# One ring of raw weight tiles for the last gate/up block and the first down group, with the forms reloaded earlier and evictions in the results' tiles

## The chip, the cores and the metric

The kernel runs on 1 core of one Trainium2 chip. The metric is the device time of one execution in microseconds. Before the change it is 1963.46 us, the median of 3 runs (1961.62 to 1964.4).

## The reference, cut to what matters

The input is one sequence of 512 tokens by 2048 features in float32. The layer is an input projection, two attention mixers, an output projection, and then a SwiGLU feed-forward block; a final RMSNorm follows. The change touches only the feed-forward block, and its last part:

```
h2 = rmsnorm(x, g_ffn[layer])
gate, up = jnp.split(jnp.einsum('bsd,df->bsf', h2, w_gate_up[layer]), 2, axis=-1)
x = x + jnp.einsum('bsf,fd->bsd', jax.nn.silu(gate) * up, w_down[layer])
```

`w_gate_up` is 2048 by 11264 and `w_down` 5632 by 2048, both float32.

## The kernel before

**Arithmetic.** A float32 product is made of three matmuls on rounded halves (L227 to L229: high by high, high by low, low by high). So each weight tile needs a high part, which ACT writes (L836), and a low part, which DVE writes as the tile less its high part (L839). Large products use a seven-product scheme: of four blocks of weights it makes seven combinations, called forms, m1 to m7, worked through in the order m1, m7, m6, m2, m5, m4, m3. The combinations of weights are sums on DVE (L972, here called the sum). The activations' forms lie in two tiles that stay in SBUF, `arena2` (two forms) and `arena5` (five).

**Gate/up.** Eleven blocks, each of 56 units: 7 forms by 8 units, where a unit is six matmuls. Two units share one sum and one split, and are called a duo here. So a form has the duos 0 to 3. A block loads 28 raw weight tiles of 512 KB by SyncE's queue (L272). They are named here by form and duo: a0 to a3 (for m1), c0, b0, ..., c3, b3 (m7; m6 is made of the same tiles), d0 to d3 (m2), e0 to e3 (m5, which sums e with a), f0 to f3 (m4, which sums f with b), g0 to g3 (m3). The eight tiles a and b stay in SBUF from m1 or m7 to m5 or m4, since these sums are written into them.

**Rings.** The raw tiles of gate/up block 1 to 9 come from a ring of 12 places, tag `craw`: a place goes to the next raw tile in the order in which places came free. A raw place is free when the split to its low part (L839) or the sum that read it (L972) is done. Block 10, the last one, has a ring of its own with 10 places, tag `craw40`, and the first down group another of 10 places, tag `draw6`.

**Loading.** The kernel is planned unit by unit: `prepare(n)` stands ahead of unit n, and issues loads (`load_raws`), high splits, sums and low splits as far ahead as rings and times allow. All weight loads go in the order of their use on one queue, so a load that waits holds the loads behind it.

**Results of a gate/up block.** Products are copied (`snap`), added (L1228), passed through SiLU and multiplied; the outcome is transposed by DMA (L1257), merged by ACT into a tile `pair` (L1263), summed there by DVE into forms (L378), and stored to DRAM by GpSimd's queue (L1266, 896 KB, in two halves per block). The second half of block 9 is stored in block 10, and the second half of block 10 in the first down group. In block 10 these results lie in general slots, in the other blocks in tiles of their own.

**Down.** Three groups of weight rows (6, 8 and 8 pairs), each by two column blocks. In group 1 a column block has 42 units and 24 raw loads; its loads are named D.0, D.1 and so on here. `next_forms` brings the activations' forms back from DRAM ahead of each group: a load on ACT's queue (L1306, 512 KB for four pairs), a high split on ACT (L1309) and a low split on DVE (L1312), each form's at a turn counted in units. An eviction copies a result bank with ACT (L1333) and adds it to DRAM by a GpSimd DMA (L1334). Its tiles are a ring of six, tag `ev`.

Of the kernel before, what the change touches and what calls it, by code (L numbers as in the profile page):

```python
# [11 lines left out]
F32 = mybir.dt.float32  # L12
# [8 lines left out]
P = 128  # L21
# [4 lines left out]
KD = D // P  # L26
# [23 lines left out]
SPILLED = {"A": 4, "B": 6}  # L50
TWINS = 8
WIDE = 4
WIDE_AHEAD = 9.5
RAWS = {"raw": 6, "craw": 12, "craw1": 24, "craw0": 24, "kraw": 9, "craw40": 10, "draw6": 10, "draw8": 15}
KEPT_TAGS = ("craw",)
W_TILES = {"wi": 10, "wo": 12}
DOWN_PAIRS = (6, 8, 8)
ORDER = ("m1", "m7", "m6", "m2", "m4", "m5", "m3")
# [1 line left out]
EVICT = 6  # L60
# [15 lines left out]
def encoder_block(ctx, tc, x, w_in, g_q_a, g_k_a, w_out, w_gate_up, w_down, g_final, x_t, gains, c_ident, c_mask,  # L76
# [15 lines left out]
    def slot(base, dtype=F32, shape=(P, 512)):  # L92
        return sp.tile(list(shape), dtype, tag="s", name=nm(base))
# [25 lines left out]
    stage = wp.tile([P, 20, 512], F32, tag="stage", bufs=1, name="stage")  # L119
    homes = deque(stage[:, n] for n in range(8, 20))  # L120
    homing = [True]
    kept_raws = deque()
    extra_homes, retired = {}, []

    def more_homes(name, tile):
# [109 lines left out]
    twins, evs, frs = [], [], []  # L235
# [965 lines left out]
    held = {}  # L1201

    def hold(name, shape, dtype=F32):
        if name not in held:
            held[name] = sp.tile([P] + list(shape), dtype, tag=name, bufs=1, name=nm(name))
        return held[name]

    forms_dram = dp.tile([P, 7, NFF // 2, 256], F32, tag="forms", name="forms")
    def gate_up_block(f0):
        box = ColBlock(w_gate_up, 0, (f0 * P, DFF + f0 * P), KD // 2, REREAD, "craw40" if f0 == 40 else "craw", hf if f0 == 0 else None, two=True)  # L1210
        st = {}

        def tile2(name):
            st[name] = [slot(name) if f0 == 40 else hold(f"{name}{t}", [512]) for t in range(2)]
            return st[name]

        def snap(form, name):
# [60 lines left out]
        for n, late in enumerate((3, 4, 6, 7)):  # L1278
            box.after("m3", late, lambda n=n: planes(("glo", "uhi")[n // 2], n // 2, n % 2))
            box.after("m3", late + 7, lambda n=n: turn(n))  # L1280
        for j, late in enumerate((23, 50 if f0 == 40 else 36)):
            for n, part in enumerate(((1, 0, 4, 1024), (0, 2, 4, 0), (0, 0, 2, 256))):
                box.after("m3", late + n, lambda j=j, part=part: merge(j, *part))
            box.after("m3", late + 3, lambda: pair_sums(hpart[0]))
            box.after("m3", late + 5, lambda j=j: store(f0 // 2 + j))
        return box

    for f in range(0, NFF, 4):
        box = gate_up_block(f)

    def load_x1(c, rows):
        for t in rows:
# [3 lines left out]
    def next_forms(box, first, pairs):  # L1296
        seq, turns = sorted(CHAIN, key=box.at.get), [0]

        def ready(form, h):
            m, st = ORDER.index(form), {}  # L1300
            lo_q, n = 4 * h, min(4, pairs - 4 * h)
            hi, lo = (form_tile(m, slice(lo_q, lo_q + n))[:, :, j] for j in range(2))

            def load():
                st["t"] = in_turn(frs, 2, [P, 4, 256], F32, "fr")[:, :n]
                nc.scalar.dma_start(st["t"], forms_dram[:, m, first + lo_q:first + lo_q + n])  # L1306

            def split_hi():
                nc.scalar.activation(hi, st["t"], AF.Copy)  # L1309

            def split_lo():
                nc.vector.tensor_tensor(lo, st["t"], f32(hi), op=OP.subtract)  # L1312
            turn = max(box.at[form] + 4 * seq.index(form) + 4 * h + 1, turns[-1] + 4)
            turns.append(turn)
            hook(turn - 5, load)
            hook(turn, split_hi)
            hook(turn + 2, split_lo)
        for form in seq:
            for h in range(-(-pairs // 4)):
                ready(form, h)  # L1320
# [3 lines left out]
    def down_block(first, pairs, cb, last):  # L1324
# [3 lines left out]
        def add(form, i, j):  # L1328
            def go():
                for t in range(2):  # L1330
                    row = 2 * i + t
                    e = in_turn(evs, EVICT, [P, 512], F32, "ev")
                    nc.scalar.activation(e, box.bank_of(form)[t], AF.Copy, scale=r2["r"][:, row:row + 1])  # L1333
                    nc.gpsimd.dma_start(x1_dram[2 * cb + j, row], e, accum_op=OP.add)  # L1334
                if form in LAST_OF_BANK:
                    box.done(form)
            box.after(form, 0, go)
# [129 lines left out]
    def load_raws(n):  # L1467
        while done["load"] < len(units) and at[done["load"]] <= at[n] + units[done["load"]].load_ahead:
            for raw in units[done["load"]].raws:
                if raw.t is None:  # L1470
                    for r in live:
                        if last_use[r] < done["lo"] and r.homed and homing[0] and not any(r.t is h for h in retired):
                            homes.append(r.t)
                        elif last_use[r] < done["lo"] and not homing[0] and r.tag in KEPT_TAGS:
                            kept_raws.append(r.t)
                    live[:] = [r for r in live if last_use[r] >= done["lo"]]
                    if homing[0] and len(homes) <= (2 if xs[KD - 1] is None else 4 if done["load"] < 24 else 0):
                        return
                    if homing[0] and raw.tag == "raw" and sum(r.tag == "raw" for r in live) >= 2:
                        return  # L1480
                    if sum((r.tag == "raw") == (raw.tag == "raw") for r in live) >= RAWS[raw.tag]:
                        return
                    live.append(raw)
                    raw.load()
            done["load"] += 1
# [115 lines left out]
```

## Time and profile before

| | us |
|---|---|
| median of 3 runs | 1963.46 |
| the profiled execution | 1962.45 |
| its span | 1960.7 |
| TensorE busy in it | 1940.9 |
| VectorE busy in it | 1537.2 |
| ScalarE busy in it | 1129.3 |

The mean granted clock was 0.996. The first matmul of gate/up block 9 starts at 1368.07 us of the span, of block 10 at 1444.23, of the first column block of down group 1 at 1526.21, of its second at 1583.37, and of down group 2 at 1647.16. Matmuls overlap in the records, so that a unit's length is read from start to start. A weight load row (`raw`) starts at its issue; the chain of waits counts it until it lands.

### The profile page before, as it was taken

Reading aid. Unit: us, or ns where it says so; the run is one execution under the profiler, and the core shown is the slowest. Engines: PE = TensorE matmul, PEld = TensorE weight load, DVE = VectorE, ACT = ScalarE, POOL = GpSimd, SP = SyncE. Lnnn points to the kernel's source line nnn. Section 1 sums busy time; section 2 is a strip of 40 time slices with the busy share of each in tenths; the row PEclk is TensorE's granted clock in tenths of the full one; section 3 lists DMA queues with packets and bytes.
Section 4 is the critical chain, followed back from the end, with each engine's and each line's share of the span. In section 5 each row is a group of like instructions: output and inputs, shape, how many; then the busy total and the mean of one; then the engine's idle time right before and its main releaser. Section 6 shows DMA issues by size and latency. Waiting matters only on the chain.

```text
span 1960.7 us, 24582 instructions
## 1 busy us (share of the span) xinstructions
PE 1940.9 (99%) x8727; PEld 1600.7 (82%) x8727; DVE 1537.2 (78%) x2012; ACT 1129.3 (58%) x1649; POOL 140.2 (7%) x184
## 2 busy tenths in 40 slices
PE   9999999999999999999999999999999999999998
PEld 7888888888888888888888888888887887888886
DVE  7987778887775697778778778778787877787886
ACT  7655554565455565555555555555555656555555
POOL 1000011000000000000000000000000121111121
PEclk9999999999999999999999999999999999999999
DMA  9777693144342466858758757767678789868865
GB/s 345 236 258 236 210 280 108 59 145 156 102 151 97 172 209 188 295 150 274 262 151 284 242 173 278 224 197 283 200 231 288 202 220 296 225 157 252 225 146 167
DMA packets 256252, 410.35 MB, mean 209 GB/s; under 512 B 62912, under 2 KB 90048, under 8 KB 256000
## 3 DMA queue, kind: packets, MB, share of 16 engines
q1 hardware_dynamic: 225296, 322.17, 50.5%
q0 software_dynamic: 22480, 60.57, 12.4%
q10 hardware_dynamic: 8352, 26.05, 4.0%
q8 instruction: 68, 1.11, 0.2%
q14 instruction: 56, 0.46, 0.1%
HBM read 334.52 MB, written 62.65 MB: 203 GB/s over the span
## 4 chain that ended last, share of the span: by engine, by line
PE 91%; DVE 4%; issue 2%; DMA 2%; ACT 1%; POOL 0%; SPq 0%; DVEq 0%; POOLq 0%; ACTq 0%
PE b L229 29%; PE b L228 29%; PE b L227 29%; PE b L612 1%; DMA raw<-in_w_gate_up_dram 1%; DVE wide L839 1%; POOL x1d L1334 0%; PE b L1170 0%; DVE raw L972 0%; PE b L562 0%; DMA forms<-pair 0%; DMA raw<-in_w_in_dram 0%; DVE x L1124 0%; DMA raw<-in_w_down_dram 0%; DVE w L305 0%
## 5 line engine op out<-in xcount | busy, mean ns | idle before, releaser
L836 ACT ACTIVATE wide<-raw 128x1024 fp32r<-128x1024 f32 x462 | 487.2, 1059 | 474.3 <-PE b L229 265.7
L228 PE MATMUL b<-wide,arena 128*128 128x512 f32 x1848 | 721.4, 390 | 4.4 <-DVE wide L839 4.4
L227 PE MATMUL b<-wide,arena 128*128 128x512 f32 x1848 | 721.2, 390 | 3.1 <-ACT wide L836 2.5
L839 DVE TENSOR_TENSOR wide<-raw,wide 128x1024 fp32r<-128x1024 f32 x462 | 562.5, 1223 | 205.2 <-ACT wide L836 195.7
L229 PE MATMUL b<-wide,arena 128*128 128x512 f32 x1848 | 721.0, 390 | 0.0
L228 PEld LDWEIGHTS b<-wide,arena 128*128 128x128 f32 x1848 | 347.9, 188 | 77.8 <-DVE wide L839 5.6
L227 PEld LDWEIGHTS b<-wide,arena 128*128 128x128 f32 x1848 | 348.0, 188 | 76.0 <-ACT wide L836 2.9
L229 PEld LDWEIGHTS b<-wide,arena 128*128 128x128 f32 x1848 | 348.0, 188 | 72.6
L972 DVE TENSOR_TENSOR raw<-raw,raw 128x1024 f32<-128x1024 f32 x264 | 321.5, 1220 | 11.9 <-DMA raw<-in_w_gate_up_dram 11.8
L228 PE MATMUL b<-tw,arena 128*128 128x512 f32 x396 | 154.3, 390 | 0.6 <-DVE tw L895 0.6
L229 PE MATMUL b<-tw,arena 128*128 128x512 f32 x396 | 154.2, 389 | 0.0
L227 PE MATMUL b<-tw,arena 128*128 128x512 f32 x396 | 154.1, 389 | 0.0
L892 ACT ACTIVATE tw<-stage 128x512 fp32r<-128x512 f32 x140 | 85.5, 628 | 69.4 <-DVE stage L972 45.0
L895 DVE TENSOR_TENSOR tw<-stage,tw 128x512 fp32r<-128x512 f32 x140 | 93.9, 688 | 22.0 <-ACT tw L892 21.2
L218 ACT ACTIVATE pTh<-b 128x512 fp32r<-128x512 f32 x64 | 38.2, 597 | 101.0 <-PE b L612 95.7
L227 PE MATMUL b<-w,arena 128*128 128x512 f32 x240 | 95.8, 399 | 0.0
L229 PE MATMUL b<-w,arena 128*128 128x512 f32 x240 | 93.9, 391 | 0.0
L228 PE MATMUL b<-w,arena 128*128 128x512 f32 x240 | 93.5, 390 | 0.0
L1334 POOL DMA_DIRECT2D x1d<-ev x76 | 66.0, 962 | 318.0 <-ACT ev L1333 295.3
L378 DVE TENSOR_TENSOR pair<-pair 128x256 f32<-128x256 f32 x120 | 46.6, 422 | 53.6 <-ACT pair L1263 29.4
L228 PEld LDWEIGHTS b<-tw,arena 128*128 128x128 f32 x396 | 74.3, 188 | 16.8 <-DVE tw L895 1.5
L229 PEld LDWEIGHTS b<-tw,arena 128*128 128x128 f32 x396 | 74.3, 188 | 15.8 <-DVE arena L346 0.4
(229 smaller groups left out, 2107.0 us busy)
## 6 DMA issues: line engine op xcount, KB each, us to landing
raw<-in_w_gate_up_dram SPq DMA_DIRECT2D x308, 512.0 KB, 6.1
raw<-in_w_down_dram SPq DMA_DIRECT2D x88, 512.0 KB, 6.9
stage<-in_w_in_dram SPq DMA_DIRECT2D x111, 256.0 KB, 5.3
forms<-pair POOLq DMA_DIRECT2D x22, 896.0 KB, 8.2
x1d<-ev POOLq DMA_DIRECT2D x76, 256.0 KB, 6.2
fr<-forms ACTq DMA_DIRECT2D x35, 512.0 KB, 6.2
raw<-in_w_out_dram SPq DMA_DIRECT2D x32, 512.0 KB, 4.2
stage<-in_w_in_dram SPq DMA_DIRECT2D x90, 128.0 KB, 3.4
```

What stands on the lines that cost most here:

```text
L218: nc.scalar.activation(hi, src, AF.Copy)
L227: nc.tensor.matmul(dst, ah, bh, start=start, stop=False, skip_group_check=chained)
L228: nc.tensor.matmul(dst, ah, bl, start=False, stop=False, skip_group_check=chained)
L229: nc.tensor.matmul(dst, al, bh, start=False, stop=stop, skip_group_check=chained)
L378: nc.vector.tensor_tensor(out, x, y, op=op)
L612: nc.tensor.transpose(ps[:, t * P:(t + 1) * P], self.p[t][:, kb * P:(kb + 1) * P], ident)
L836: nc.scalar.activation(self.hi, self.src, AF.Copy)
L839: nc.vector.tensor_tensor(self.lo, self.src, f32(self.hi), op=OP.subtract)
L892: nc.scalar.activation(self.pair[:, 0], self.src, AF.Copy)
L895: nc.vector.tensor_tensor(self.pair[:, 1], self.src, f32(self.pair[:, 0]), op=OP.subtract)
L972: nc.vector.tensor_tensor(t[dst], t[src[0]], t[src[1]], op=OP.add if form == "m6" else OP.subtract)
L1334: nc.gpsimd.dma_start(x1_dram[2 * cb + j, row], e, accum_op=OP.add)
```

## The change

The last block and down group 1 take their raw tiles from the ring `craw` too, which is 12 places at first and 10 from unit 22 of block 10 on: two places that come free then are dropped. The results of every block lie in the results' own tiles (`s1`, `s7`, `s6` and so on, each of two halves), and the evictions use the six halves of `s1`, `s6` and `s7` in place of the ring `ev`. The first group's forms are reloaded from unit 24 of block 10 on at the earliest, every four units. The second merge of block 10 stands 40 units behind the start of m3's evictions, not 50. The ring `draw8` has 16 places instead of 15.

```diff
+RELOAD_AT = 24
+RELOAD_STEP = 4
+DROP_AT = 22
-RAWS = {"raw": 6, "craw": 12, "craw1": 24, "craw0": 24, "kraw": 9, "craw40": 10, "draw6": 10, "draw8": 15}
-KEPT_TAGS = ("craw",)
+RAWS = {"raw": 6, "craw": 12, "craw1": 24, "craw0": 24, "kraw": 9, "craw40": 10, "draw6": 10, "draw8": 16}
+KEPT_TAGS = ("craw", "craw40", "draw6")
...
-    kept_raws = deque()
+    kept_raws, dropped = deque(), [0]
...
-            st[name] = [slot(name) if f0 == 40 else hold(f"{name}{t}", [512]) for t in range(2)]
+            st[name] = [hold(name, [2, 512])[:, t] for t in range(2)]
...
-        for j, late in enumerate((23, 50 if f0 == 40 else 36)):
+        for j, late in enumerate((23, 40 if f0 == 40 else 36)):
...
+    last_gate = box.at["m1"] - KD // 2 + 1
...
             turn = max(box.at[form] + 4 * seq.index(form) + 4 * h + 1, turns[-1] + 4)
+            if first == 0:
+                turn = max(box.at[form] + 1, box.at["m1"] + RELOAD_AT, turns[-1] + RELOAD_STEP)
...
-                    e = in_turn(evs, EVICT, [P, 512], F32, "ev")
+                    if not evs:
+                        evs.extend(held[name][:, t] for name in ("s1", "s6", "s7") for t in range(2))
+                    evs.append(evs.pop(0))
+                    e = evs[-1]
...
-                            kept_raws.append(r.t)
+                            if n >= last_gate + DROP_AT and dropped[0] < RAWS["craw"] - RAWS["draw6"]:
+                                dropped[0] += 1
+                            else:
+                                kept_raws.append(r.t)
...
-                    if sum((r.tag == "raw") == (raw.tag == "raw") for r in live) >= RAWS[raw.tag]:
+                    most = RAWS["craw"] if raw.tag == "craw40" and n < last_gate + DROP_AT else RAWS[raw.tag]
+                    if sum((r.tag == "raw") == (raw.tag == "raw") for r in live) >= most:
```

The number of instructions on each engine stays the same, and so does the order on TensorE and SyncE. Lines of the kernel's body stand three to eleven lower after the change: L272, L839 and L972 become L275, L842 and L975, L1266 becomes L1269, L1312 becomes L1317, and L1334 becomes L1344.

The first place is the weight loads on SyncE in m2 and m5 of block 10. Before, these eight rows are the loads d2, d3, e0, e1, e2, e3, f0 and f1; every raw tile has a name of its own, and the pool gives it its place.

```order
L272 DMA raw_571_10949<-in_w_gate_up_dram 128x2x512
L272 DMA raw_572_10967<-in_w_gate_up_dram 128x2x512
L272 DMA raw_575_10990<-in_w_gate_up_dram 128x2x512
L272 DMA raw_576_11012<-in_w_gate_up_dram 128x2x512
L272 DMA raw_577_11031<-in_w_gate_up_dram 128x2x512
L272 DMA raw_578_11033<-in_w_gate_up_dram 128x2x512
L272 DMA raw_579_11050<-in_w_gate_up_dram 128x2x512
L272 DMA raw_580_11052<-in_w_gate_up_dram 128x2x512
```

After the change the same eight loads on SyncE go to tiles of the ring, so a name that comes again is a place used again.

```order
L275 DMA raw_518_5788<-in_w_gate_up_dram 128x2x512
L275 DMA raw_534_5886<-in_w_gate_up_dram 128x2x512
L275 DMA raw_539_5961<-in_w_gate_up_dram 128x2x512
L275 DMA raw_534_5886<-in_w_gate_up_dram 128x2x512
L275 DMA raw_536_5908<-in_w_gate_up_dram 128x2x512
L275 DMA raw_539_5961<-in_w_gate_up_dram 128x2x512
L275 DMA raw_512_5739<-in_w_gate_up_dram 128x2x512
L275 DMA raw_534_5886<-in_w_gate_up_dram 128x2x512
```

The place of d2 (`raw_518`) is not used again, and e1 goes where d3 was (`raw_534`), e2 to the place of a0 (`raw_536`), into which the sum of e0 is written, e3 to e0's place (`raw_539`), f0 to a1's (`raw_512`), f1 to e1's.

The second place is DVE in the same stretch. Before the change this is what stands there, from the sum of e0 (out in a0's tile, `raw_551`) to the split of e2's sum.

```order
L972 TENSOR_TENSOR raw_551_10632<-raw_575_10990,raw_551_10632 128x1024
L839 TENSOR_TENSOR wide_532_5847<-raw_572_10967,wide_531_5846 128x1024
L1312 TENSOR_TENSOR arena2_84<-fr_562_10790,arena2_84 128x2x256
L972 TENSOR_TENSOR raw_552_10648<-raw_576_11012,raw_552_10648 128x1024
L839 TENSOR_TENSOR wide_526_5841<-raw_551_10632,wide_525_5840 128x1024
L972 TENSOR_TENSOR raw_553_10664<-raw_577_11031,raw_553_10664 128x1024
L839 TENSOR_TENSOR wide_528_5843<-raw_552_10648,wide_527_5842 128x1024
L972 TENSOR_TENSOR raw_554_10680<-raw_578_11033,raw_554_10680 128x1024
L839 TENSOR_TENSOR wide_530_5845<-raw_553_10664,wide_529_5844 128x1024
```

After the change DVE has this there, again from the sum of e0 (out in `raw_536`) on.

```order
L975 TENSOR_TENSOR raw_536_5908<-raw_539_5961,raw_536_5908 128x1024
L842 TENSOR_TENSOR wide_532_5847<-raw_534_5886,wide_531_5846 128x1024
L975 TENSOR_TENSOR raw_512_5739<-raw_534_5886,raw_512_5739 128x1024
L842 TENSOR_TENSOR wide_526_5841<-raw_536_5908,wide_525_5840 128x1024
L975 TENSOR_TENSOR raw_538_5940<-raw_536_5908,raw_538_5940 128x1024
L842 TENSOR_TENSOR wide_528_5843<-raw_512_5739,wide_527_5842 128x1024
L975 TENSOR_TENSOR raw_537_5938<-raw_539_5961,raw_537_5938 128x1024
L842 TENSOR_TENSOR wide_530_5845<-raw_538_5940,wide_529_5844 128x1024
```

The low split of d3 (out of `raw_534`) is the second row, and e1 (third row) comes into that same tile behind it; the split of e0's sum (fourth row) is the last reader of `raw_536` before e2 is loaded there, and the sum of e2 is the row behind. The reload (L1312) between the first rows is gone from here. Further on in the same stretch, DVE after the change has these rows, from the split of f2's sum (`raw_524`) to that of g0:

```order
L842 TENSOR_TENSOR wide_530_5845<-raw_524_5838,wide_529_5844 128x1024
L1231 TENSOR_TENSOR s7_545_6137<-b7_78,s7_545_6137 128x512
L1231 TENSOR_TENSOR s7_545_6137<-b6_77,s7_545_6137 128x512
L1317 TENSOR_TENSOR arena2_84<-fr_548_10972,arena2_84 128x4x256
L842 TENSOR_TENSOR wide_532_5847<-raw_535_5906,wide_531_5846 128x1024
L842 TENSOR_TENSOR wide_526_5841<-raw_537_5938,wide_525_5840 128x1024
```

Before the change the two adds of this place (L1228) are followed by the split of f3's sum with no reload (L1312) between. The third place is GpSimd's queue at the turn from the first to the second column block of down group 1, where the store of the last forms stood among the evictions like this:

```order
L1334 DMA x1d11_127<-ev_598_11376 128x512
L1334 DMA x1d20_130<-ev_599_11377 128x512
L1334 DMA x1d21_131<-ev_600_11378 128x512
L1334 DMA x1d32_136<-ev_601_11379 128x512
L1334 DMA x1d33_137<-ev_602_11380 128x512
L1266 DMA forms_138<-pair_467_5381 896x1x256
```

After the change the same stretch of GpSimd's queue reads:

```order
L1344 DMA x1d11_127<-s1_544_6071 128x512
L1269 DMA forms_138<-pair_467_5381 896x1x256
L1344 DMA x1d20_130<-s6_546_6203 128x512
L1344 DMA x1d21_131<-s6_546_6203 128x512
L1344 DMA x1d32_136<-s7_545_6137 128x512
L1344 DMA x1d33_137<-s7_545_6137 128x512
```

The store of the `pair` tile now stands ahead of the first two evictions of the second column block. In this column block the load D.22 went to the place of `pair` before (tile `raw_615`); now it goes to the ring's `raw_538`, which the low split of the sum of a down unit reads last, and D.24 is the first load at a place of the next group's ring.

## The prediction

> **What bounds the kernel now.** I read the page's first part, then the busy time by block, TensorE's waits, and the chain of waits around the two places where it waits. The page, and TensorE's waits summed over the run (us in total, times, longest):
>
> ```profile
> span 1960.7 us, 24582 instructions
> PE 1940.9 (99%) x8727; PEld 1600.7 (82%) x8727; DVE 1537.2 (78%) x2012; ACT 1129.3 (58%) x1649; POOL 140.2 (7%) x184
> ...
> PE b L228 <- DVE wide L839: 4.4, 3, 3.5
> PE b L227 <- ACT wide L836: 2.5, 1, 2.5
> ```
>
> TensorE is the bound. Only time in which it waits, or runs at a lower clock, can be gained. The same by stage, from the start of one block's matmuls to the next: block 10, the two column blocks of down group 1, and block 9 as a block without waits (the eighth column is the granted clock):
>
> ```profile
> core 0: us, PE busy (x) PEld busy (x) DVE busy (x) ACT busy (x) POOL busy (x), PEclk, DMA share, GB/s
> 1444.23:1526.21 81.98, 78.34 (x338) 64.06 (x336) 67.97 (x72) 48.97 (x56) 1.81 (x2) 0.98 0.82 260
> 1526.21:1583.37 57.16, 57.16 (x254) 47.24 (x252) 47.11 (x47) 39.63 (x47) 7.96 (x9) 1.00 0.80 212
> 1583.37:1647.16 63.79, 60.57 (x253) 49.32 (x252) 45.94 (x44) 38.82 (x46) 16.45 (x19) 0.95 0.92 246
> 1368.07:1444.23 76.16, 76.16 (x338) 63.07 (x336) 60.18 (x63) 43.02 (x48) 1.82 (x2) 1.00 0.68 218
> ```
>
> Block 10 does block 9's matmuls and takes 81.98 - 76.16 = 5.82 us longer; the second column block takes 63.79 - 57.16 = 6.63 us longer than the first. All that the changed stretch can give is 12.45 us. A unit takes 76.16 / 56 = 1.36 us. How the loss in block 10 arises, from the chain of waits (start, us, what), and the same for the second column block behind the dots:
>
> ```profile
> 1482.61 6.55 DMA raw<-in_w_gate_up_dram
> 1489.18 1.24 DVE raw L972
> 1490.43 3.63 DMA raw<-in_w_gate_up_dram
> ...
> 1609.32 5.97 DMA forms<-pair
> 1615.54 4.61 DMA raw<-in_w_down_dram
> 1620.23 1.06 ACT wide L836
> ```
>
> In block 10 the load e1 is issued at 1482.61 and lands at 1489.16; DVE takes e1's sum (m5's duo 1) ahead of the low split of duo 0, so TensorE waits for that split until 1491.59. In the second column block D.22 may be issued only when the store of `pair` has landed, at 1615.3, since it goes to that place; SyncE's waits (us in total, times, longest) have this as one wait, and TensorE's and DVE's timelines show what follows:
>
> ```profile
> SPq L272 <- DMA forms<-pair: 37.5, 1, 37.5
> ...
> 1489.18 1.22 DVE L972 TENSOR_TENSOR raw<-raw,raw 128x1024 f32<-128x1024 f32 x1 [4.86 <-DMA raw<-in_w_gate_up_dram]
> 1490.32 1.22 DVE L839 TENSOR_TENSOR wide<-raw,wide 128x1024 fp32r<-128x1024 f32 x1
> 1491.69 1.23 DVE L972 TENSOR_TENSOR raw<-raw,raw 128x1024 f32<-128x1024 f32 x1
> ...
> 1491.59 0.50 PE L228 MATMUL b<-wide,arena 128*128 128x512 f32 x1 [3.46 <-DVE wide L839]
> ...
> 1621.34 0.50 PE L227 MATMUL b<-wide,arena 128*128 128x512 f32 x1 [2.45 <-ACT wide L836]
> 1622.60 0.79 PE L228 MATMUL b<-wide,arena 128*128 128x512 f32 x1 [0.76 <-DVE wide L839]
> ```
>
> After each wait the clock is lower for a while (granted clock, eighth column, over 5 us slices):
>
> ```profile
> 1490.00:1495.00 5.00, 3.41 (x9) 2.68 (x10) 4.82 (x5) 2.11 (x2) 0.00 (x0) 0.73 0.84 271
> 1620.00:1625.00 5.00, 2.90 (x7) 2.10 (x8) 3.01 (x3) 4.75 (x6) 0.00 (x0) 0.70 1.07 271
> 1625.00:1630.00 5.00, 5.00 (x16) 3.92 (x15) 4.07 (x5) 2.73 (x4) 1.72 (x2) 0.62 1.05 392
> ```
>
> So the 6.63 us are 2.45 + 0.76 = 3.21 of waiting, and 3.42 of slow clock.
>
> **The change, part by part.** *Second column block.* The load D.22 leaves the place of `pair` for a ring place, whose last reader is a low split on DVE. Before, the split of that down unit is the row at 1606.90 here, done at 1608.1:
>
> ```profile
> 1606.90 1.22 DVE L839 TENSOR_TENSOR wide<-raw,wide 128x1024 fp32r<-128x1024 f32 x1
> ```
>
> The load could then leave 7.4 us earlier than 1615.5. At 4.61 us it lands at 1612.7; ACT needs it at about 1618.7 - 1.06 = 1617.6, since unit 26 of this column block would start at 1583.37 + 26 x 1.36 = 1618.7. That is 4.9 us of cover. The store itself, four evictions earlier on GpSimd's queue, is moved by ten units of 1.36, about 13.6 us; the first load that waits for it now is D.24, and that stands behind D.22 on SyncE's queue, which leaves at 1608.1 at the earliest, after a landing at about 1615.3 - 13.6 = 1601.7. Gain 6.63, both the wait and the clock. Its bounds are 0 and 6.63.
>
> *Block 10.* With two places dropped after unit 22, two are left beside the eight kept tiles, as before. What differs is who frees them. Before, e1 waits for the sum of e0, e2 for the low split of d3, e3 for the sum of e1. Now e1 waits for the split of d3, which stands one DVE instruction of 1.14 us behind the sum of e0; the reload between is gone (0.6), so e1 leaves at about 1483.4 instead of 1482.61. What it costs to be beside the store of block 9's second half, from two DMA answers: a load issued 1.7 us behind such a store in block 9, and the load e1 itself, which also had a form's load from ACT's queue beside it (issues, KB, us to landing):
>
> ```profile
> 1405.28 0.91 POOL L1266 DMA_DIRECT2D forms<-pair  x1 [56.10 <-DVE pair L378]
> 1482.08 0.91 POOL L1266 DMA_DIRECT2D forms<-pair  x1 [56.55 <-DVE pair L378]
> ...
> raw<-in_w_gate_up_dram SPq DMA_DIRECT2D x1, 512.0 KB, 5.1
> ...
> raw<-in_w_gate_up_dram SPq DMA_DIRECT2D x1, 512.0 KB, 6.5
> fr<-forms ACTq DMA_DIRECT2D x1, 512.0 KB, 7.2
> ```
>
> So e1 lands between 1488.5 and 1489.9; e2 no longer runs beside it. I take 1489.2, as before: the start of m5, which I call T, stays 1491.6 (landing, sum, split: 2.4). Its bounds are 3.6 and 7.2 us for e1, so T from 1489.4 to 1493.
>
> Now e2 waits for the split that ends at T, where before it was in flight already when the split ran (its sum starts at 1491.69, right behind). A load alone took 3.63 us (the chain's third row above). DVE is strictly in order, and the sum of e2 is its next row, so DVE stands still for 3.7 us, and behind it wait the splits of every later duo. That is the first term. Its bounds are 3.6 and 4.6 (the last is D.22's row). From there to the split of f2's sum DVE has six sums (e2 to f3) and six splits (of e1's sum to f2's) at 1.14, two adds, four pair sums and reloads of 1.14 and 0.60, all from these rows:
>
> ```profile
> 1496.36 1.28 DVE L1228 TENSOR_TENSOR s<-b,s 128x512 f32<-128x512 f32 x2
> 1497.56 1.22 DVE L972 TENSOR_TENSOR raw<-raw,raw 128x1024 f32<-128x1024 f32 x1
> 1498.69 1.22 DVE L839 TENSOR_TENSOR wide<-raw,wide 128x1024 fp32r<-128x1024 f32 x1
> 1499.83 1.22 DVE L1312 TENSOR_TENSOR arena<-fr,arena 128x1024 fp32r<-128x1024 f32 x1
> ...
> 1505.50 1.55 DVE L378 TENSOR_TENSOR pair<-pair 128x256 f32<-128x256 f32 x4
> 1506.97 0.68 DVE L1312 TENSOR_TENSOR arena<-fr,arena 128x512 fp32r<-128x512 f32 x1
> 1508.71 1.22 DVE L839 TENSOR_TENSOR wide<-raw,wide 128x1024 fp32r<-128x1024 f32 x1
> 1509.84 1.28 DVE L1228 TENSOR_TENSOR s<-b,s 128x512 f32<-128x512 f32 x2
> ```
>
> 12 x 1.14 + 1.2 + 1.5 + 1.7 = 18.1. Before, the same work ran from 1491.69 to 1509.9, which is 18.2: the sum holds, and TensorE was caught by it there at unit 44, which nominally starts at 1444.23 + 44 x 1.36 = 1504.1. Now that split ends at T + 3.7 + 18.1 = T + 21.8. Then come two adds (1.2), a reload that stood elsewhere before (1.14), and the split of f3's sum (1.14): T + 25.3, where TensorE's unit 46 can start. Before, adds and split were 2.3 and fitted into the duo's 2.72; now 3.5 do not: a second term of 0.8, which is 0 if DVE has caught up there. The other loads do not bind: e3 leaves right behind e2, f0 at T + 6.1 and is wanted at T + 10.6, f2 at T + 8.3 and is wanted at T + 15.8. Unit 46 would nominally start at 1506.8, and starts at 1516.9: block 10 loses 10.1 us instead of 5.82, that is +4.3. From m3 on one DVE split per duo and no sums remain, and TensorE is the bound again. A slow clock costs nothing extra here: from T to T + 25.3 TensorE has 14 units of 1.36, 19.0, and so 6.3 to spare, more than the 3.42 above. With the bounds of T (-2.2 to +1.4), of e2's load (to +1.0) and of the reload (to -0.8), the stage costs +1.3 to +6.7.
>
> The sum: +4.3 - 6.63 = -2.3. The profiled execution had 1962.45 us (span 1960.7, and 1.75 around it), which gives 1960.1; the median of the runs, 1963.46, lies 1.0 above it, and I forecast 1961.2.
>
> *At nothing:* the results' own tiles and the evictions in six halves of them are as many tiles as before, and GpSimd's queue is busy 16.45 of 63.79 us in the densest stage above; a late eviction would cost first on ACT, which has 25 us idle there. The reloads' counts stay. The ring of 16 in groups 2 and 3 covers stages in which TensorE does not wait now.
>
> *A rule against the row.* The slow clock after D.22's wait came after 2.45 us of idle, one matmul and 0.76 us more. The Trainium skill's page "TensorE: Matmul & The Clock Gate" says, under "What's actually happening", that the clock halves after an idle window of about 3.4 us, which 3.21 us would not fill. By that rule the slow clock there is not the wait's doing, and the sum is the one of the rival below. The trace does not agree: the rows at 0.70 and 0.62 stand right behind the wait.
>
> **Rivals.** *The early loads get through (faster).* If e1 lands in 3.6 us because the store's packets are done by then, T is 1489.4 and the sum is -2.3 - 2.2 = -4.5: 1959.0. The row of 6.5 us at the same place speaks against. If besides e2 found a free place before T, block 10 would lose what it does in block 9, nothing: -5.82 - 6.63 = -12.45, 1951.0. The order of the tiles speaks against: e2 goes where e0's sum lies.
>
> *D.22 is late all the same (slower).* From a row of the second column block: six loads issued from 1615.4 on with two accumulates beside them took this long (median).
>
> ```profile
> raw<-in_w_down_dram SPq DMA_DIRECT2D x6, 512.0 KB, 11.0
> ```
>
> If the queue behind the late block 10 is so crowded that D.22 takes over 9.5 us (1608.1 to 1617.6), the wait comes back: at 11 us it is 1.5, with a slow clock as before it keeps 1.5 + 3.4 of the 6.63. Then the time is 1963.46 + 4.3 - 1.7 = 1966.1, and 1967.8 if all of it stays. That the loads were so slow since they were all held up to 1615.5 and then left together speaks against it.
>
> *The slow clock stays.* If it came from something else at that place, only the 3.21 of waiting goes: +4.3 - 3.21 = +1.1, 1964.6. The rows behind the wait speak against.
>
> *Nothing changes.* The ring may hand out places so that e1 and e2 overlap as before, and D.22 waits for another late reader. Both losses stay: 1963.5.
>
> **How the numbers follow.** Forecast 0.58, of which 0.08 lies below -0.2% through the bounds of T, 0.02 above +0.2%. Early e1 0.13; no loss in block 10 0.05; D.22 late 0.13; the slow clock stays 0.04; nothing changes 0.07. A measurement of this kernel can tell about 0.2%, 3.9 us, from no change. Faster: 0.08 + 0.13 + 0.05 = 0.26; slower 0.02 + 0.13 = 0.15; the same 0.48 + 0.04 + 0.07 = 0.59. The forecast's own bounds are 1963.46 + 1.3 - 6.63 = 1958.1 and 1963.46 + 6.7 - 6.63 = 1963.5. The range goes from 1957.0, which takes in the early e1, to 1966.0, the lower end of the late D.22; the case at 1951 and most of the late one are left out.
>
> **What would show it.** Right: D.22 issued near 1608 plus block 10's shift, no TensorE wait in the second column block and 57.2 us for it; in block 10 one more DVE idle of about 3.7 us ahead of e2's sum, released by a raw load, and 86.3 us for the block. Wrong: e2 landed before the split ahead of it was done, a wait in the first column block, or a wait on the forms' reload.

## The result, and the profile after

Over 20 runs of each kernel the median is 1966.01 us after the change (1962.92 to 1971.48) and 1962.74 before (1960.59 to 1964.4). The ratio is 1.0019, with a 95% interval from 1.0012 to 1.0026: slower by some 3 us, and not faster by 2.3. The profiled execution after the change has a span of 1964.2 us. Its page, and TensorE's waits summed over the run (us in total, times, longest):

```profile
span 1964.2 us, 24572 instructions
PE 1942.3 (99%) x8727; PEld 1600.9 (82%) x8727; DVE 1536.8 (78%) x2012; ACT 1128.3 (57%) x1649; POOL 140.2 (7%) x184
...
PE b L231 <- DVE wide L842: 8.9, 5, 3.8
...
PE b L230 <- ACT s L1343: 0.4, 1, 0.4
```

Waits for DVE's low splits have doubled (4.4 before), and the wait of 2.5 for ACT in the second column block is gone. The last line, 0.4 for an eviction's copy on ACT, is new. By stage, from start to start: block 10, and the two column blocks of down group 1 (the eighth column is the granted clock):

```profile
1445.78:1533.90 88.12, 80.80 (x337) 64.78 (x336) 65.38 (x69) 47.08 (x54) 1.81 (x2) 0.96 0.67 216
1533.90:1593.57 59.67, 57.71 (x254) 47.14 (x252) 49.32 (x50) 41.64 (x50) 10.60 (x12) 1.00 0.84 219
1593.57:1650.69 57.12, 57.12 (x254) 47.30 (x252) 46.55 (x44) 37.67 (x45) 13.83 (x16) 1.00 1.01 276
```

Against before, block 10 loses 88.12 - 81.98 = 6.14 us, the first column block loses 59.67 - 57.16 = 2.51, and the second gains 63.79 - 57.12 = 6.67. That is +1.98. A further 1.55 of the 3.5 by which the two spans differ lies ahead of block 10 (1445.78 against 1444.23), and is there by 62 us of the span. Ahead of that, the pace differs in the first ten microseconds. This is a slice of 5 us there, before the change, after it, and in the run e1 below, whose work up to block 10 is that of before; the number in brackets behind the first busy time counts matmuls:

```profile
5.00:10.00 5.00, 4.76 (x21) 3.97 (x22) 3.44 (x6) 2.94 (x5) 0.71 (x1) 1.00 1.02 359
```

```profile
5.00:10.00 5.00, 4.97 (x12) 3.97 (x13) 3.30 (x5) 2.70 (x5) 0.71 (x1) 1.00 1.00 336
```

```profile
5.00:10.00 5.00, 5.00 (x15) 3.98 (x16) 3.27 (x5) 2.70 (x5) 0.71 (x1) 1.00 1.03 356
```

The clock column reads 1.00 in all three, so the pace is read from the matmuls: the same twelve, from about 5 us on, took 3.00 us before the change, 5.18 after it and 4.67 in e1. TensorE starts up at a slow pace for a time that differs from execution to execution; block 10 starts anywhere from 1444.1 to 1446.3 in the profiles of this study. So profiles are compared by stage here, and the medians tell the sum.

Where block 10's time went is seen in the timelines of DVE and TensorE after the change (start, us, engine, line, operation; in brackets the idle time before and what ended it):

```profile
1483.41 1.22 DVE L842 TENSOR_TENSOR wide<-raw,wide 128x1024 fp32r<-128x1024 f32 x1
1491.07 1.22 DVE L975 TENSOR_TENSOR raw<-raw,raw 128x1024 f32<-128x1024 f32 x1 [6.44 <-DMA raw<-in_w_gate_up_dram]
1492.21 1.22 DVE L842 TENSOR_TENSOR wide<-raw,wide 128x1024 fp32r<-128x1024 f32 x1
1498.05 1.23 DVE L975 TENSOR_TENSOR raw<-raw,raw 128x1024 f32<-128x1024 f32 x1 [4.62 <-DMA raw<-in_w_gate_up_dram]
...
1510.17 0.69 DVE L1317 TENSOR_TENSOR arena<-fr,arena 128x512 fp32r<-128x512 f32 x1 [0.62 <-ACT arena L1314]
...
1493.48 0.50 PE L231 MATMUL b<-wide,arena 128*128 128x512 f32 x1 [3.79 <-DVE wide L842]
1500.46 0.50 PE L231 MATMUL b<-wide,arena 128*128 128x512 f32 x1 [2.38 <-DVE wide L842]
```

Before, DVE stood still once here (4.86 us, for e1). Now it does so twice: 6.44 us for e1, and 4.62 for e2, which was issued only when the split of e0's sum was done at 1493.4. In the first column block a chain now reaches TensorE, in ACT's, DVE's and TensorE's timelines (the loads D.0 to D.23 are those of the whole of group 1, twelve to a column block, so D.11 is the last of the first):

```profile
1559.04 1.06 ACT L1314 ACTIVATE arena<-fr 128x1024 fp32r<-128x1024 f32 x1 [2.04 <-DMA fr<-forms]
...
1570.99 1.06 ACT L839 ACTIVATE wide<-raw 128x1024 fp32r<-128x1024 f32 x1 [0.64 <-DMA raw<-in_w_down_dram]
...
1572.66 1.22 DVE L381 TENSOR_TENSOR pair<-pair 128x256 f32<-128x256 f32 x3 [2.81 <-ACT pair L1266]
1573.80 1.22 DVE L1317 TENSOR_TENSOR arena<-fr,arena 128x1024 fp32r<-128x1024 f32 x1
1574.94 1.22 DVE L975 TENSOR_TENSOR raw<-raw,raw 128x1024 f32<-128x1024 f32 x1
1576.07 2.43 DVE L842 TENSOR_TENSOR wide<-raw,wide 128x1024 fp32r<-128x1024 f32 x2
...
1577.34 0.50 PE L231 MATMUL b<-wide,arena 128*128 128x512 f32 x1 [1.55 <-DVE wide L842]
```

ACT stands 2.04 us for a form's reload, later 0.64 for the weight load D.11, which leaves 29.8 us into the column block and not 25.1 as before; its last merge part stands behind D.11's split, DVE's pair sums wait 2.81 us for that merge, and the low split that TensorE wants (1576.07) stands behind the pair sums, a reload and a sum. TensorE's 0.41 us for an eviction, at 1561.68, comes of the same 2.04 us on ACT, and lies ahead of this longer wait. Before, the same stretch of ACT's and DVE's timelines was this:

```profile
1561.90 1.06 ACT L836 ACTIVATE wide<-raw 128x1024 fp32r<-128x1024 f32 x1 [2.81 <-DMA raw<-in_w_down_dram]
...
1563.57 1.22 DVE L378 TENSOR_TENSOR pair<-pair 128x256 f32<-128x256 f32 x3 [4.02 <-ACT pair L1263]
1564.71 1.22 DVE L972 TENSOR_TENSOR raw<-raw,raw 128x1024 f32<-128x1024 f32 x1
1565.84 1.22 DVE L839 TENSOR_TENSOR wide<-raw,wide 128x1024 fp32r<-128x1024 f32 x1
1566.97 1.22 DVE L1312 TENSOR_TENSOR arena<-fr,arena 128x1024 fp32r<-128x1024 f32 x1
```

ACT waited for D.11 and the pair sums for ACT then too, and longer, but the pair sums started 37.4 us into the column block, and now 38.8; and the reload stood behind the split, where it now stands ahead of it.

### The profile page after: what moved, and what is told of

Same layout as the page of the kernel before. It is cut to its first block, busy times and chain, and to the rows that moved or that the text cites. A ratio compares the mean times of both kernels' runs of the same rounds, so it can differ in the third digit from the quotient of the medians.

```text
span 1964.2 us, 24572 instructions
## 1 busy us (share of the span) xinstructions
PE 1942.3 (99%) x8727; PEld 1600.9 (82%) x8727; DVE 1536.8 (78%) x2012; ACT 1128.3 (57%) x1649; POOL 140.2 (7%) x184
## 4 chain that ended last, share of the span: by engine, by line
PE 92%; DVE 4%; DMA 1%; ACT 1%; issue 1%; SPq 0%; ACTq 0%; DVEq 0%; POOLq 0%; POOL 0%
PE b L232 30%; PE b L230 30%; PE b L231 30%; PE b L615 1%; DVE wide L842 1%; DMA raw<-in_w_gate_up_dram 1%; DVE raw L975 0%; DMA raw<-in_w_down_dram 0%; PE b L1173 0%; PE b L565 0%; DMA raw<-in_w_in_dram 0%; PE b L792 0%; DVE x L1127 0%; DVE w L308 0%; DVE ra L462 0%
## 5 line engine op out<-in xcount | busy, mean ns | idle before, releaser
L839 ACT ACTIVATE wide<-raw 128x1024 fp32r<-128x1024 f32 x462 | 486.8, 1058 | 468.9 <-PE b L232 253.3
L842 DVE TENSOR_TENSOR wide<-raw,wide 128x1024 fp32r<-128x1024 f32 x462 | 561.5, 1220 | 196.5 <-ACT wide L839 188.3
L975 DVE TENSOR_TENSOR raw<-raw,raw 128x1024 f32<-128x1024 f32 x264 | 320.8, 1217 | 18.5 <-DMA raw<-in_w_gate_up_dram 18.3
L1344 POOL DMA_DIRECT2D x1d<-s x76 | 66.0, 971 | 315.3 <-ACT s L1343 289.9
```

Source lines behind the costliest of these rows:

```text
L839: nc.scalar.activation(self.hi, self.src, AF.Copy)
L842: nc.vector.tensor_tensor(self.lo, self.src, f32(self.hi), op=OP.subtract)
L975: nc.vector.tensor_tensor(t[dst], t[src[0]], t[src[1]], op=OP.add if form == "m6" else OP.subtract)
```

## The experiments

Each run's stages are the lengths of block 10 and of the two column blocks of down group 1 in its profile, in this order. Before they are 81.98, 57.16 and 63.79, after the change 88.12, 59.67 and 57.12. From group 2 on all runs but one take what the kernel before takes.

**e1, the store alone.** The kernel of before with one number changed.

```diff
-        for j, late in enumerate((23, 50 if f0 == 40 else 36)):
+        for j, late in enumerate((23, 40 if f0 == 40 else 36)):
```

> The kernel of before, with only the second merge of block 10 at 40 units instead of 50, so that the last store of forms leaves some 13.6 us earlier. If D.22 waits for that store alone, the store lands near 1602 of the span, D.22 leaves there, the second column block of down group 1 takes 57.2 us instead of 63.8, block 10 stays at 82.0, and the time falls by 6.6 to about 1956.1 (ratio 0.9966). Rival: the wait only moves to another late reader of that place, or the earlier store collides with loads that are needed sooner: 1962 or more.

Measured: 1957.26 against 1963.27, ratio 0.9969 (0.9956 to 0.9981), some 1.2 us above what was expected. The stages, by busy time in the windows:

```profile
1445.32:1528.71 83.39, 78.68 (x337) 63.98 (x336) 67.98 (x72) 48.99 (x56) 1.81 (x2) 0.98 0.84 255
1528.71:1585.84 57.13, 57.13 (x254) 47.30 (x253) 46.13 (x46) 40.05 (x47) 9.40 (x12) 1.00 0.81 214
1585.84:1642.95 57.11, 57.11 (x253) 47.26 (x252) 46.55 (x44) 38.42 (x46) 15.00 (x18) 1.00 1.00 271
...
SPq L272 <- DMA forms<-pair: 24.3, 1, 24.3
```

The last line is from SyncE's waits: D.22 waits for the store as before, but for 24.3 us instead of 37.5, and the second column block has no wait. One number out of the whole change gives all of its gain. Block 10 took 1.4 more than before in this profile, with no work moved in it up to there: two executions can differ this far in that stage.

**e2, the ring without the store.** The changed kernel with the second merge back at 50.

```diff
-        for j, late in enumerate((23, 40 if f0 == 40 else 36)):
+        for j, late in enumerate((23, 50 if f0 == 40 else 36)):
```

> The changed kernel with the second merge back at 50 units. D.22 still goes to a ring place and D.24 is the first load that waits for the store. If the ring alone takes the wait away, the second column block stays at 57.1 us and the time at 1966. If the store's own time matters too (D.24 late, or the store beside D.22), the column block goes up to 63.8 and the time to 1972.

Measured: 1969.97, ratio 1.0033 (1.0021 to 1.0046), so neither of the two times. Windows, the last one down group 2's first column block (76.16 us without a wait):

```profile
1444.75:1532.73 87.98, 80.80 (x337) 65.01 (x336) 65.59 (x69) 47.06 (x54) 1.81 (x2) 0.96 0.68 216
1532.73:1594.78 62.05, 59.05 (x254) 48.36 (x252) 50.12 (x50) 41.12 (x49) 10.57 (x12) 0.97 0.84 218
1594.78:1651.90 57.12, 57.12 (x254) 47.30 (x252) 44.49 (x42) 33.79 (x40) 12.14 (x14) 1.00 0.92 243
...
1651.90:1732.03 80.13, 76.97 (x337) 62.86 (x336) 62.66 (x55) 48.52 (x55) 13.86 (x16) 1.00 0.88 244
```

The ring takes D.22's wait away too (57.12). But the wait for the store has only moved on to D.24, and costs 80.13 - 76.16 = 3.97 us in the next group. The first column block lost 2.4 more than after the change, in one profile: TensorE waited 3.00 us in it, and the clock was lower behind the wait (0.97 over the stage).

**e3, e2 to the place of e0.** The changed kernel; of tiles that come free together the later one goes back to the ring first.

```diff
-                    for r in live:
+                    for r in (sorted(live, key=lambda r: (last_use[r], -last_use_at[r])) if raw.tag in ("craw40", "draw6") else live):
```

> The changed kernel, but of two raw tiles that come free together the later one goes back to the ring first, so that e2 goes to e0's place (read last by the sum of e0) and e3 to a0's. Theory one, the serial load: DVE's idle time of 4.6 us ahead of the sum of e2 falls below 1.5, block 10 takes 83 to 85 us instead of 88.1, and the time is about 1962. Rival, the denser reloads cost it: block 10 stays above 87 and the time at 1965 or more.

Measured: 1963.21, ratio 1.0003 (0.9994 to 1.0012). Stages 86.75, 57.85 and 58.23: block 10 fell by 1.4 where 3 to 5 were expected. DVE's timeline tells why:

```profile
1493.84 1.22 DVE L975 TENSOR_TENSOR raw<-raw,raw 128x1024 f32<-128x1024 f32 x1
1494.97 1.22 DVE L842 TENSOR_TENSOR wide<-raw,wide 128x1024 fp32r<-128x1024 f32 x1
1499.50 1.23 DVE L975 TENSOR_TENSOR raw<-raw,raw 128x1024 f32<-128x1024 f32 x1 [3.31 <-DMA raw<-in_w_gate_up_dram]
```

The idle time ahead of the sum of e2 (first row) is gone as expected, but e3 now goes to a0's place, and DVE waits 3.31 us for it. With two spare places, mending one link moves the wait to the next.

**e4, two places more until unit 30.** The changed kernel with one number changed.

```diff
-DROP_AT = 22
+DROP_AT = 30
```

> The changed kernel with the two places dropped from unit 30 of block 10 on instead of 22. e1, e2 and e3 then wait for the splits of d1, d2 and d3 only. Theory one: all three land before they are wanted, block 10 takes 76 to 79 us instead of 88.1, and the time is about 1956; if the 2.5 us in the first column block are carried over from block 10's lateness they go as well, and the time is 1953.5. Rival, the denser reloads: block 10 stays above 80 and the first column block at 59.7.

Measured: 1957.38, ratio 0.9969 (0.9956 to 0.9982). The first two stages, and DVE's only wait for a weight load there:

```profile
1444.35:1523.24 78.89, 77.37 (x337) 62.75 (x336) 64.81 (x68) 46.94 (x54) 1.82 (x2) 1.00 0.76 241
1523.24:1582.99 59.75, 57.74 (x254) 47.14 (x252) 49.82 (x51) 41.74 (x51) 10.60 (x12) 1.00 0.83 220
...
1489.68 1.22 DVE L975 TENSOR_TENSOR raw<-raw,raw 128x1024 f32<-128x1024 f32 x1 [1.95 <-DMA raw<-in_w_gate_up_dram]
```

With four places e1 and e2 land ahead of their sums; the wait left is for e3. 9.2 of block 10's 12 us of loss go, though all the reloads stand where the change put them. The first column block still takes 59.75. So its loss isn't carried over from a late block 10.

**e5, the reload undone.** The changed kernel with the turns of before; this needs the ring at 10 places from block 10's start on.

```diff
-DROP_AT = 22
+DROP_AT = 0
...
-            if first == 0:
-                turn = max(box.at[form] + 1, box.at["m1"] + RELOAD_AT, turns[-1] + RELOAD_STEP)
```

> The changed kernel with the reload turns of before; the ring has 10 places from the start of block 10, and e1 still waits for the split of d3, e2 for the split of e0's sum. Theory one: the serial load stays (DVE idle about 4.6 us ahead of the sum of e2), two or three reloads fewer stand behind it, block 10 takes 85.5 to 87 us instead of 88.1; the denser reloads delay the split of D.0, so without them the first column block takes 57.2 instead of 59.7; time about 1962. Rival: the 2.5 us in the first column block come from the ring's places, and it stays at 59.7 and the time at 1964.5 or more.

Measured: 1964.61, ratio 1.0006 (0.9997 to 1.0015).

```profile
1446.24:1535.68 89.44, 80.86 (x338) 64.97 (x336) 68.07 (x72) 49.10 (x56) 1.82 (x2) 0.96 0.73 220
1535.68:1592.80 57.12, 57.12 (x254) 47.30 (x252) 46.49 (x47) 40.72 (x48) 10.61 (x12) 1.00 0.84 218
...
1491.96 1.23 DVE L975 TENSOR_TENSOR raw<-raw,raw 128x1024 f32<-128x1024 f32 x1 [5.61 <-DMA raw<-in_w_gate_up_dram]
1499.61 1.23 DVE L975 TENSOR_TENSOR raw<-raw,raw 128x1024 f32<-128x1024 f32 x1 [5.28 <-DMA raw<-in_w_gate_up_dram]
1507.02 1.23 DVE L975 TENSOR_TENSOR raw<-raw,raw 128x1024 f32<-128x1024 f32 x1 [1.58 <-DMA raw<-in_w_gate_up_dram]
```

Block 10 is as late as ever, and the first column block has no wait: the reload turns cause its 2.5 us. In block 10 the expectation of 85.5 to 87 failed: from the sum of e2 to the split of f3's sum DVE has two reloads in place of three, but f0's load came late instead (1.58, third row), and the loads of e2 and f0 took longer (5.2 and 5.0 us, against 4.6 and 3.9). The second column block took 58.29. In this profile the three stages add up to 204.85 us, against 204.91 after the change.

**e6, the ring undone.** The changed kernel with the pool's rings of 10.

```diff
-KEPT_TAGS = ("craw", "craw40", "draw6")
+KEPT_TAGS = ("craw",)
...
-                    most = RAWS["craw"] if raw.tag == "craw40" and n < last_gate + DROP_AT else RAWS[raw.tag]
+                    most = RAWS[raw.tag]
```

> The changed kernel with the pool's own rings of 10 for block 10 and down group 1, as before the change; reload turns, merge and results' tiles stay changed. The pool's order now lets e1 wait for the split of d2 and e2 for that of d3. Theory one: no load waits for the split of e0's sum, the first unit of m5 starts on time, block 10 takes 80 to 83 us; the denser reloads keep the first column block at 59.7; D.22 goes to the place of the forms' last tile again, but the store is early: 57.1; time about 1958. Rival, the reloads alone cost block 10 its time: 87 or more, and 1965.

Measured: 1958.12, ratio 0.9976 (0.9967 to 0.9985). Stages 81.48, 60.42 and 57.12, about as expected. The pool gives its 10 places in an order in which e2 waits for the split of d3, and block 10 is 6.6 us shorter than with the hand-made ring; the reload costs the first column block its time here too: the pair sums wait 4.88 us for the merge behind D.11's split, a reload stands behind them, and TensorE waits 2.98 us.

**e7, reloads three units apart.** As e4, but with other turns. At a step of three the load of a form into one of the two `fr` tiles goes ahead of the low split that reads the tile, so that low parts are made of another form's data: that part of the computation is changed.

```diff
-DROP_AT = 22
+DROP_AT = 30
...
-RELOAD_STEP = 4
+RELOAD_STEP = 3
...
-                turn = max(box.at[form] + 1, box.at["m1"] + RELOAD_AT, turns[-1] + RELOAD_STEP)
+                turn = max(box.at[form] + 4 * seq.index(form) + 4 * h + 1, box.at["m1"] + RELOAD_AT, turns[-1] + RELOAD_STEP)
```

> The changed kernel with the places dropped from unit 30 on, and the reload turns the later of the turns of before and one every three units from unit 24 of block 10 on, so that the second half of the reloads stands where it stood before. Theory one: all e loads land in time, block 10 takes 79 to 80.5 us (one reload more in m5 and m4), the first column block 57.2 to 57.6 instead of 59.7, the second 57.1; time about 1955.5. Rival: the first column block stays at 59.7 whatever the turns, and the time at 1958.

Measured: 1966.52, ratio 1.0014 (1.0005 to 1.0023); stages 89.67, 57.79 and 59.04. From DVE's waits between 1480 and 1534:

```profile
DVE arena L1317 <- DMA fr<-forms: 9.9, 4, 4.2
```

The low split waits for a load that was issued just ahead of it, 9.9 us in all, so block 10's time says nothing of reloads in themselves. The first column block, with the later reloads where they stood before, is at 57.79.

**e8, the first merge earlier.** As e4, and:

```diff
-        for j, late in enumerate((23, 40 if f0 == 40 else 36)):
+        for j, late in enumerate((21 if f0 == 40 else 23, 40 if f0 == 40 else 36)):
```

> The run with the places dropped from unit 30, and in it the first merge of block 10 at 21 units instead of 23, so that its last part stands ahead of D.11's high split on ACT. Theory: the 2.6 us in the first column block come from D.11's late landing through ACT's order: merge behind D.11's split, pair sums behind the merge, the next low split behind the pair sums. Then the first column block takes 57.2 to 58 us instead of 59.75, and the time is 1955 to 1956. Rival: DVE is simply behind there, and the order of the merge changes nothing: 59.7 and 1957.4.

Measured: 1954.69, ratio 0.9960 (0.9948 to 0.9973). The two column blocks, DVE's pair sums, and D.22's load (issues, KB, us to landing):

```profile
1524.92:1582.04 57.12, 57.12 (x253) 47.30 (x252) 48.88 (x50) 41.49 (x50) 10.58 (x12) 1.00 0.84 218
1582.04:1641.10 59.06, 58.05 (x253) 47.07 (x252) 46.64 (x44) 37.68 (x45) 13.83 (x16) 1.00 1.00 290
...
1559.03 1.55 DVE L381 TENSOR_TENSOR pair<-pair 128x256 f32<-128x256 f32 x4
...
raw<-in_w_down_dram SPq DMA_DIRECT2D x1, 512.0 KB, 10.2
```

The pair sums no longer wait, and the first column block is free of loss with all reloads in place, though D.11 lands 38.0 us into it and landed at 37.0 after the change: it was ACT's order. The 1.94 that the second lost comes of D.22, whose load now takes 10.2 us; ACT's split waits 6.32 us for it.

**e9, reloads two units earlier.** As e8, with the reload turns of e7's diff at a step of four, and

```diff
-RELOAD_AT = 24
+RELOAD_AT = 22
```

> The same with the reload turns two units earlier (from unit 22, and not before the turns of before), so that of the reloads two fall later than now, as before the change. Theory: block 10 stays at 78.9 within 0.6, the first column block goes to 57.2 to 57.5; time 1954.5 to 1955.5. Rival: a reload more in m5 and m4 costs block 10 over 1 us, and the time is no better than that of the run with the merge alone.

Measured: 1957.65, ratio 0.9973 (0.9963 to 0.9984), worse than e8. Stages 79.80, 60.24 and 58.58. The first column block lost 3.1 us again, in other places than before (TensorE's waits lie 9 to 20 us into it), whose cause stays open.

**e10, the changed kernel with the first merge earlier.** The diff of e8 alone.

> The changed kernel with nothing else altered than the first merge of block 10 at 21 units instead of 23. Theory: block 10 stays at 88.1, the first column block goes from 59.7 to 57.2; the second keeps 57.1 to 59.1, since TensorE then comes to unit 26 up to 2.5 us earlier and D.22's landing has less cover; time between 1963.5 and 1965.5. Rival: the first column block's 2.5 us are block 10's lateness, and stay: 59.7 and 1966.

Measured: 1963.23, ratio 1.0005 (0.9996 to 1.0014).

```profile
1446.21:1534.28 88.07, 80.51 (x337) 64.57 (x336) 65.59 (x69) 47.07 (x54) 1.82 (x2) 0.96 0.67 216
1534.28:1591.55 57.27, 57.27 (x253) 47.22 (x252) 49.13 (x50) 41.71 (x50) 10.99 (x13) 1.00 0.88 225
1591.55:1649.11 57.56, 57.42 (x253) 47.22 (x252) 46.55 (x44) 37.67 (x45) 13.42 (x16) 1.00 0.98 279
```

The stages are as expected, and the time is 0.3 us below the expected range. A merge two units earlier takes 2.4 us off the first column block, with block 10 unaltered.

**e11, the store at 47.** As e8, with the second merge at 47 instead of 40.

> The run with the places dropped from unit 30 and the first merge at 21, and in it the second merge at 47 units instead of 40, which moves the last store by 9.5 us. D.24, the first load on the place of the forms' last tile, and the loads behind it then leave some 3 us later. Theory: D.22's landing of 10 us comes from the loads queued right behind it; it falls to 5 to 8 us, the second column block from 59.1 to 57.2 to 58, and the stages behind lose under 1 us; time 1953 to 1954.5. Rival: the loads behind D.22 do not matter (59.1 stays), or the later store costs down group 2 over 2 us as at 50 units: 1955.5 or more.

Measured: 1955.03, ratio 0.9959 (0.9945 to 0.9973), the same as e8. In the profile the second column block has 57.20 us, and D.22's load took 5.8. But the store landed soon enough that D.24 left 2.9 us behind D.22, as it did in e8, so the loads behind D.22 are not shown to be the cause, and the medians do not tell the two kernels apart. Why D.22 takes 5.8 us in one and 10.2 in the other stays open. One thing goes with it in the nine profiles in which D.22 goes to a ring place with an eviction's DMA beside it: by and large, the earlier GpSimd issues that DMA, the longer D.22 takes.

| | eviction's issue, behind D.22's (us) | D.22's load (us) | second column block over 57.1 (us) |
|---|---|---|---|
| e7 | -0.2 | 10.2 | 1.9 |
| e8 | -0.1 | 10.2 | 1.9 |
| e9 | 0.1 | 9.7 | 1.5 |
| e5 | 0.3 | 9.5 | 1.2 |
| e3 | 0.1 | 9.4 | 1.1 |
| e10 | 0.4 | 8.7 | 0.4 |
| after the change | 0.4 | 8.1 | 0.0 |
| e4 | 0.5 | 6.8 | 0.0 |
| e11 | 0.7 | 5.8 | 0.1 |

No run moved that eviction alone, so it is a candidate, and not shown to be the cause.

## Why the prediction was wrong

**The second column block was right in its wait, and lucky in its cover.** It was to fall to 57.2 and fell to 57.12, and D.22 waits for DVE alone. e1 and e2 add that the change holds two remedies for one wait, each sufficient for this stage: the store's time does it without the ring, and the ring without the store's time, only that the wait then comes back in group 2. The 4.9 us of cover for D.22's landing were not there. They rested on a load of 4.61 us and on a landing that could wait until 1617.6, 34.2 us into the column block. D.22's load took 8.1 us, and the table under e11 puts the limit earlier than 9.5 us: D.22 leaves 23.3 or 23.4 us into the column block (24.0 in e11), a load of 8.1 costs nothing, and 8.7, 9.4 and 10.2 us cost 0.4, 1.1 and 1.9. So what a load takes over some 8.3 us, an estimate from these rows, is lost in full, and the profile after the change stayed 0.2 us under that.

The slow clock went with the wait (1.00 in the third window after the change), as the rows of before had it. The Trainium skill's page "TensorE: Matmul & The Clock Gate" has, under "What's actually happening", the clock halve after an idle window of about 3.4 us. By that rule the slow clock of before was not the wait's doing, and would have stayed; the runs do not agree. A wait of 2.38 us, at 1500.46 after the change, was also followed by a lower clock (0.82 from 1503 to 1508). But the length of a wait alone doesn't decide it: behind the 2.98 us in e6's first column block the clock stayed at 1.00, and behind the 3.00 in e2's it was 0.68 from 1576 to 1581. What decides it is not shown.

**Block 10 was right in its mechanism, and mis-sized.** The forecast was +4.3, the profile has +6.14 (the block took 88.12 us, and 87.98 and 88.07 in e2 and e10, which leave it as it is). The serial wait of e2 stands where it was put, and e4 shows that the two dropped places cause it: with them kept for the e loads, block 10 falls to 78.89. The first term, DVE idle ahead of e2's sum, was taken from a lone load (3.7) and measured 4.62, because e3 leaves right behind e2 and shares the way; the prediction had e3 leave there, and still took the lone load. In e4, where e3 left 6.5 us behind it, e2's load took 3.6. e1 landed somewhat later, so that m5 starts 47.7 us into the block and not 47.4. The third piece, 0.62, is a reload on DVE waiting for ACT. Together 0.9 + 0.3 + 0.6 are 1.8, which is the miss. The forecast's second term, the reload of 0.8, is not tested on its own: with the reloads moved away (e5) block 10 got no shorter, but the next load bound there instead.

**The first column block was where the forecast failed.** Its step said that the reloads' counts stay, and priced the moved reloads at nothing there. That was a count over both stages, not an order. The turns of before have eight of the fourteen low splits of reloads in block 10 and six in the first column block, the new ones six and eight, every four units; a reload on ACT waits for its form's load, the split that frees D.11's place comes later and so does D.11, and through ACT's order its landing holds the merge, the pair sums and a split. The low split that TensorE waits for ended 1567.06 - 1526.21 = 40.85 us into the column block before, 0.2 us ahead of its use at 1567.24, and now ends 43.4 us into it: 1.4 by the later pair sums and 1.14 by the reload ahead of it. e5 (turns undone, 57.12), e8 and e10 (merge moved ahead of D.11's split, 57.12 and 57.27) show the cause from both sides; e4 excludes block 10's lateness, and so does e10, where block 10 is as late as ever. Two of the signs that the prediction named for being wrong came with it: a wait in the first column block, and waits on the forms' reload.

With +6.14, +2.51 and -6.67 the sum is +2.0 by stages. Of the 4.3 us between that and the forecast of -2.3, 2.5 are this step and 1.8 the size of block 10. Between the medians +3.3 were measured. The rest is within what single profiles differ by: e1's block 10 alone moved by 1.4.

**The rivals.** The early e1 did not happen: it landed 6.3 us after its issue. The late D.22 did not happen in the changed kernel's profile, but does in six of the runs (e3, e5, e7, e8, e9 and e10), at 0.4 to 1.9 us and without a slow clock, less than the 4.9 that was put on it. Its time, 1966.1, is nearly the measured one by accident, since its mechanism did not occur there. That nothing changes was wrong stage by stage, and nearer to the sum than the forecast.

## What to carry to other kernels

When a change mends one wait, look for the smallest part of it that does so: here one number, a store ten units earlier, gave 0.3%, and the rest of the change took it back. A ring given out in first-in, first-out order can chain loads to the compute that they feed: write down for each load which instruction frees its place, and count the links where spare places are fewest. Moved work isn't free because its count stays; on an engine that works in order, ask what now stands ahead of the next instruction that the bound engine wants.

The best version found is the changed kernel with the places dropped at unit 30 and the first merge at 21 (e8): 1954.69 us, 0.4% below the kernel before; e11 can't be told from it.

## What the hardware showed that I had not expected

The start-up of one and the same program up to block 10 differed by over 1 us between executions: 21, 12 and 15 matmuls in the same 5 us. A weight load of 512 KB took 3.6 us alone and 4.6 with a second one issued right behind it (e0 and e2 after the change). Two waits of TensorE of 2.98 and 3.00 us, at the same place in e6 and e2, left the clock alone once and lowered it once. The times after the change also spread over 8.6 us in 20 runs, against 3.8 before; the cause of that is open.
